# Four channel blocks of a depthwise convolution as fused multiply-adds on VectorE alone, in a two-block transformer on one core

## The chip, the core and the metric

The kernel runs on one core of a Trainium2 chip. The metric is the device time of one execution in microseconds; lower is better. A core has TensorE (PE in the rows; its weight loads are PEld), VectorE (DVE), ScalarE (ACT), GpSimd (POOL) and the queue engine SyncE (SP), each with its own queue of instructions that it works off in order, and 16 DMA engines.

## What is computed

Two transformer blocks over 256 tokens of width 1024, in float32. The second block also carries 256 context tokens, and its first mixer has attention on one half of the width and a convolution module on the other half. The change is in that module:

```python
def _conv_module(u, conv_w, conv_b, ln_g, ln_b):
    a, gate = jnp.split(u, 2, axis=-1)
    glu = a * jax.nn.sigmoid(gate)
    y = lax.conv_general_dilated(glu, conv_w[:, None, :], window_strides=(1,),
                                 padding=[(CONV_WIDTH // 2, CONV_WIDTH // 2)],
                                 dimension_numbers=('NWC', 'WIO', 'NWC'),
                                 feature_group_count=B_WIDTH) + conv_b
    ...
    return jax.nn.silu(yn)
```

The convolution is depthwise: each of 512 channels has 31 weights (CONV_WIDTH) of its own, over the 256 tokens. Then follow a layer norm over the channels and a silu. It is done once for x and once for the context.

## The kernel before, in words

Matrix products run as three float32r matmuls: both operands are split into a high and a low part, and hi*hi, hi*lo and lo*hi are summed in PSUM. Weights come through a ring of 1 MB buffers. `Splits.emit` (L281) splits 128x1024 values of weight at a time: ScalarE makes the high part (L300), VectorE subtracts it for the low part (L301); four such split buffers are in use in turn. A matmul on the low part waits for L301.

The stages around the change are these. The first block's second feed-forward layer (`ffn`, L1009) runs 8 chunks: `gemm_T` (L354, matmuls L363 to L365) makes the hidden layer, `gemm` (L306, matmuls L319 to L321) the output, which is added to x by L1040 on VectorE at the end. Between its chunks the function `between` (L2440) already projects the context for the second block's first mixer, class `MixerAB`: its gate, the other half `a` of the gated unit, keys and values, queries. `MixerAB.a` (L1287) makes the gated input GT (L1292) and calls `conv(1)` for the context. After the feed-forward layer x is normed (L456 to L490), `MixerAB.run` (L1385) projects x in the same way, with attention of the context beside it, and `a` calls `conv(0)` for x. Then come the queries and keys of x with their norm and rotation (L390 to L402, L1091 to L1105, L1111, L1127, L1134), attention (scores L1165, row maximum L1176, exponential L1183, transposes L788), and `gated_out` (L1213), which multiplies attention's output and the convolution's by the output weights and needs both.

Channels lie on the partitions, 128 to a block, so a convolution is 4 blocks (k) of 31 taps (j). `tap` (L1304) does one tap of one block over 128x256. The first tap is on ScalarE for all blocks (L1308). A later tap of a block of the engine "vector" is one scalar_tensor_tensor on VectorE (L1310): y = GT*w + y, the weight being one value per partition. A later tap of a block of the engine "gpsimd" is two instructions: ScalarE scales GT into one of four buffers (L1313) and GpSimd adds that to y (L1314).

```python
CONV = ((0.65, 0.8, 3), (0.4, 0.7, 2))
...
def conv(self, s):
    dve, pool, n = CONV[s]
    self.spare.share = dict(vector=dve, gpsimd=pool)
    for e, ks in (("vector", range(n)), ("gpsimd", range(n, 4))):
        for j in range(31):
            for k in ks:
                self.spare.add(e, 0.1 if j == 0 else 0.4 if e == "vector" else 0.7,
                               lambda k=k, j=j, e=e: self.tap(s, k, e, j))
        self.spare.add(e, 0.0, lambda: self.half(s))
```

The table CONV (L31; first entry x, second the context) gives the shares of the two engines and n, the number of blocks on VectorE: 3 of 4 for x, 2 of 4 for the context. The taps are put on two lists in `Spare` (L1192). They go into the engines' queues beside the matmuls: the generating code calls `tick` every few matmuls, a tick counts as 1.3 units of time (2.0 while it only waits, and 1.0 more where a step of attention was taken), and `Spare.step` gives each list that time multiplied by its share as credit and takes taps off it while the credit is above zero, at 0.4 a tap for VectorE and 0.7 for GpSimd. So a share sets how many taps stand between two other instructions. When both lists of a stream are done, `lnorm` (L1331) is started: transposes of y (L1339), moments (L1345), scaling (L1353), transposes back (L1362), silu (L1369 to L1373) and the split into hi and lo (L1377, L1378) for the output product, each step some ticks after the one before (STEP: 1 for x, 3 for the context).

Of the kernel before, what the change touches and what calls it, by code (L numbers as in the profile page):

```python
# [27 lines left out]
RINGS = (4, 3, 1)  # L28
OVER = 7
EXTRA = (1, 0)  # L30
CONV = ((0.65, 0.8, 3), (0.4, 0.7, 2))  # L31
STEP = (1, 3)


# [93 lines left out]
def body(tc, d, dump=None):  # L128
    nc = tc.nc
    es = ExitStack()  # L130
    with es:
# [1100 lines left out]
        class MixerAB:  # L1232
# [83 lines left out]
# [9 lines that stand above are left out]
# [1218 lines left out]
```

## Time and profile before

| | us |
|---|---|
| median of 3 runs (2215.06 to 2218.03) | 2217.5 |
| the profiled execution, its own time | 2219.68 |
| its span, first to last instruction | 2217.9 |
| TensorE busy | 2010.5 (91%) |
| VectorE busy | 1037.8 (47%) |
| ScalarE busy | 773.9 (35%) |
| GpSimd busy | 487.4 (22%) |

Times in rows are microseconds from the span's start; ns where marked or where a mean of one instruction is given. A busy share over the whole span is an average over stages with different limits. In a row of the table by stage the pairs are busy time and number of instructions, in the order TensorE, weight loads, VectorE, ScalarE, GpSimd; the granted clock is the share of TensorE's full clock that it was given. A row of a group names line, engine, operation, the tile written and the tiles read, the shape and the count; then busy time and mean of one; then the idle time of the engine just before such instructions and what ended it. In the timeline, "x7" are seven instructions run one after the other in the length given; an idle time before them stands in brackets with its releaser.

### The profile page before, as it was taken

How to read it: one execution, taken by the hardware profiler on the slowest of the kernel's cores; microseconds unless marked ns; L12 is line 12 of the kernel's file. 1: busy time of each engine (PE TensorE's matmuls, PEld its weight loads, DVE VectorE, ACT ScalarE, POOL GpSimd, SP SyncE). 2: the span in 40 equal slices, each digit the busy share in tenths (PEclk: the TensorE clock that was granted, in tenths of full speed). 3: DMA queues.
4: the chain of work that ended last, by engine and by line, in shares of the span. 5: the costliest groups of instructions: out<-in, count | busy, mean ns of one | idle time of the engine just before them, and what ended most of it. 6: DMA issues, size and time to landing. Idle time of an engine off the chain costs nothing. (4 is left out here: it accounts for less than half of the span.)

```text
span 2217.9 us, 28427 instructions
## 1 busy us (share of the span) xinstructions
PE 2010.5 (91%) x10991; PEld 1273.2 (57%) x10991; DVE 1037.8 (47%) x2033; ACT 773.9 (35%) x1379; POOL 487.4 (22%) x443
## 2 busy tenths in 40 slices
PE   7998999997998798579899998999798799998998
PEld 5765888774898686357444454444375534443333
DVE  5744554654658955875633232333463422222222
ACT  5544544555666556554211111111264311111110
POOL 3000110100115610403232332332340111111111
PEclk8998999998999998788999999999999899999999
DMA  9775677675554342114699997999742699999998
GB/s 321 271 262 202 237 249 258 208 266 173 176 194 152 126 159 78 56 48 161 236 420 414 411 413 298 416 416 412 279 152 109 236 420 421 421 421 383 421 421 340
DMA packets 160766, 613.00 MB, mean 276 GB/s; under 512 B 10527, under 2 KB 16255, under 8 KB 111344
## 3 DMA queue, kind: packets, MB, share of 16 engines
q1 hardware_dynamic: 155744, 596.86, 69.9%
q0 software_dynamic: 4448, 13.51, 2.2%
q8 instruction: 89, 1.46, 0.3%
q10 hardware_dynamic: 432, 0.74, 0.1%
q14 instruction: 53, 0.43, 0.1%
HBM read 607.90 MB, written 3.16 MB: 276 GB/s over the span
## 5 line engine op out<-in xcount | busy, mean ns | idle before, releaser
L1966 PE MATMUL acc<-w,XT 128*64 128x512 f32 x1856 | 437.2, 600 | 18.8 <-DVEq L2233 10.7
L301 DVE TENSOR_TENSOR w<-w 128x1024 fp32r<-128x1024 f32 x244 | 307.0, 1271 | 193.8 <-ACT w L300 172.5
L300 ACT ACTIVATE w<-w 128x1024 fp32r<-128x1024 f32 x252 | 265.0, 1059 | 184.8 <-PE acc L321 93.2
L1966 PEld LDWEIGHTS acc<-w,XT 128*64 128x64 f32 x1856 | 139.0, 138 | 282.6 <-issue 253.5
L2025 POOL TENSOR_TENSOR X<-X,tm 128x512 f32<-128x512 f32 x124 | 155.3, 1280 | 424.9 <-DVE tm L2023 424.9
L2023 DVE TENSOR_TENSOR tm<-acc,gate 128x512 f32<-128x512 f32 x196 | 129.6, 686 | 217.9 <-PE acc L2013 172.2
L2004 PE MATMUL acc<-w,hT 128*64 128x512 f32 x912 | 215.8, 598 | 6.0 <-ACT hT L1992 6.0
L363 PE MATMUL acc<-hi,w 128*128 128x256 f32 x576 | 166.4, 289 | 8.1 <-ACT qn L1102 3.8
L364 PE MATMUL acc<-lo,w 128*128 128x256 f32 x576 | 164.1, 285 | 0.8 <-POOL lo L490 0.8
L365 PE MATMUL acc<-hi,w 128*128 128x256 f32 x576 | 164.0, 285 | 0.6 <-DVE w L301 0.6
L321 PE MATMUL acc<-w,lo 128*128 128x512 f32 x368 | 150.6, 409 | 1.8 <-POOL lo L1378 1.6
L319 PE MATMUL acc<-w,hi 128*128 128x512 f32 x336 | 143.5, 427 | 7.0 <-ACT hi L1377 5.5
L320 PE MATMUL acc<-w,hi 128*128 128x512 f32 x336 | 137.6, 409 | 9.8 <-DVE w L301 9.8
L2025 POOL TENSOR_TENSOR C<-C,tm 128x512 f32<-128x512 f32 x64 | 79.5, 1275 | 273.8 <-DVE tm L2023 273.8
L1992 ACT ACTIVATE hT<-trp 128x512 f32<-128x512 f32 (+1 forms) x33 | 19.6, 592 | 329.3 <-PE trp L1989 329.3
L1983 DVE SCALAR_TENSOR_TENSOR hd<-sg,ws,acc 128x512 f32<-128x512 f32 (+1 forms) x33 | 36.3, 1100 | 195.9 <-issue 99.4
L2004 PEld LDWEIGHTS acc<-w,hT 128*64 128x64 f32 x912 | 62.7, 136 | 110.5 <-issue 99.0
L363 PEld LDWEIGHTS acc<-hi,w 128*128 128x128 f32 x576 | 111.3, 193 | 10.8 <-ACT qn L1102 4.0
L1314 POOL TENSOR_TENSOR cy<-cy,tap 128x256 f32<-128x256 f32 x90 | 88.1, 998 | 120.0 <-ACT tap L1313 70.6
L365 PEld LDWEIGHTS acc<-hi,w 128*128 128x128 f32 x576 | 112.5, 195 | 0.8 <-DVE w L301 0.8
L2136 PE MATMUL acc<-P,hi 128*128 128x256 f32 x544 | 104.5, 291 | 8.9 <-issue 6.6
L364 PEld LDWEIGHTS acc<-lo,w 128*128 128x128 f32 x576 | 111.4, 193 | 1.4 <-POOL lo L490 1.1
(425 smaller groups left out, 3521.3 us busy)
## 6 DMA issues: line engine op xcount, KB each, us to landing
w<-in_ex_gate_dram SPq DMA_DIRECT2D x118, 1024.0 KB, 13.3
w<-in_ex_up_dram SPq DMA_DIRECT2D x118, 1024.0 KB, 14.3
w<-in_ex_down_dram SPq DMA_DIRECT2D x118, 1024.0 KB, 13.1
w<-in_ffn_w_dram SPq DMA_DIRECT2D x64, 1024.0 KB, 5.2
fw<-in_mod_w_dram SPq DMA_DIRECT2D x48, 1024.0 KB, 7.5
w<-in_a_w_qkv_dram SPq DMA_DIRECT2D x17, 1024.0 KB, 10.3
w<-in_w_in_ab_dram SPq DMA_DIRECT2D x14, 1024.0 KB, 5.3
w<-in_b_w_qkv_dram SPq DMA_DIRECT2D x12, 1024.0 KB, 5.7
```

The costliest lines, as they stand in the source:

```text
L300: nc.scalar.activation(wh, w, AF.Copy)
L301: self.engine.tensor_tensor(wl, w, wh.bitcast(F32), op=OP.subtract)
L319: nc.tensor.matmul(ps[:, :n], xh, wh, start=first, stop=False)
L320: nc.tensor.matmul(ps[:, :n], xh, wl, start=False, stop=False)
L321: nc.tensor.matmul(ps[:, :n], xl, wh, start=False, stop=last)
L363: nc.tensor.matmul(z, wh[:, js], xh, start=k == 0 and j % 2 == 0, stop=False)
L364: nc.tensor.matmul(z, wh[:, js], xl, start=False, stop=False)
L365: nc.tensor.matmul(z, wl[:, js], xh, start=False, stop=k == 7 and j % 2 == 1)
L1966: nc.tensor.matmul(p[self.rows(a)], self.XT[:, 4 * k0 + k, self.rows(a)], units[v + a][:, k], start=k0 + k == 0, stop=4 * k0 + k == 7)
L2004: nc.tensor.matmul(self.p[c][self.rows(a)], self.hT[:, 2 * n + k, self.rows(a)], units[v + a][:, k, s], start=n + k == 0, stop=n + k == 2)
L2023: nc.vector.tensor_tensor(g, p, gates[s][:, c], op=OP.mult)
L2025: add.tensor_tensor(dst, dst, g, op=OP.add)
```

## The change

It alters the table of shares and nothing else in the source: all four blocks are put on VectorE's list, GpSimd's list holds only the call that counts it as done, and VectorE's share goes from 0.65 to 0.85 for x and from 0.4 to 0.5 for the context.

```diff
-CONV = ((0.65, 0.8, 3), (0.4, 0.7, 2))
+CONV = ((0.85, 0.1, 4), (0.5, 0.1, 4))
```

With it the 90 instructions of L1313 and the 90 of L1314 are gone, and 90 of L1310 come in. What the new shares do to the order shows in three places.

GpSimd's queue, from the context's gated input to the output product (L1025 squares the hidden layer, L490 and L1378 split, L674 loads gates, L1220 adds the output to the stream):

```order
 L1290 MEMSET GT 128x4x15
-L1314 TENSOR_TENSOR cy<-cy,tap 128x256 x11
-L1025 TENSOR_TENSOR s<-r 128x512 x2
-L1314 TENSOR_TENSOR cy<-cy,tap 128x256 x26
-L1025 TENSOR_TENSOR s<-r 128x512 x2
-L1314 TENSOR_TENSOR cy<-cy,tap 128x256 x23
-L1025 TENSOR_TENSOR s<-r 128x512 x2
```

The 60 adds of the context leave the queue, and the squares follow one another; the 30 of x go in the same way.

VectorE's queue in the last chunks of the feed-forward layer, after the second query tile of the context (L1088), where before the context's last two FMAs and then only splits stood:

```order
 L1088 TENSOR_TENSOR qr<-qn,gain_5311 128x2x4x64
 L301 TENSOR_TENSOR w<-w 128x1024
+L1310 SCALAR_TENSOR_TENSOR cy<-GT,cols,cy 128x256 x3
+L301 TENSOR_TENSOR w<-w 128x1024
+L1310 SCALAR_TENSOR_TENSOR cy<-GT,cols,cy 128x256 x3
+L301 TENSOR_TENSOR w<-w 128x1024
+L1310 SCALAR_TENSOR_TENSOR cy<-GT,cols,cy 128x256 x3
+L301 TENSOR_TENSOR w<-w 128x1024
+L1310 SCALAR_TENSOR_TENSOR cy<-GT,cols,cy 128x256 x5
+L1031 TENSOR_TENSOR hl<-s,hh 128x512
```

Up to the place of the context's last FMA before there are now 76 FMAs in place of 60; the other 44 go between the splits of the rest of the layer, one to five at a time, and the layer norm of the context (L1345 and on) moves behind the first addition into x (L1040).

VectorE's queue in the stretch of x, around the second query tile:

```order
-L1310 SCALAR_TENSOR_TENSOR cy<-GT,cols,cy 128x256 x6
+L1310 SCALAR_TENSOR_TENSOR cy<-GT,cols,cy 128x256 x9
 L586 TENSOR_REDUCE hss<-qr 128x8
 L390 TENSOR_SCALAR nv<-hss 128x8
 L301 TENSOR_TENSOR w<-w 128x1024
-L1310 SCALAR_TENSOR_TENSOR cy<-GT,cols,cy 128x256 x3
+L1310 SCALAR_TENSOR_TENSOR cy<-GT,cols,cy 128x256 x4
 L397 RECIPROCAL rstd<-sd 128x8
```

Each burst of FMAs between the other instructions of that stretch is longer by up to three; 13 of the 30 more stand before the place that ran at 944, 17 after it.

## Rows read from the trace of the kernel before

**Rows 1.** the page, part 1: busy time, share of the span, instructions of each engine.

```profile
PE 2010.5 (91%) x10991; PEld 1273.2 (57%) x10991; DVE 1037.8 (47%) x2033; ACT 773.9 (35%) x1379; POOL 487.4 (22%) x443
```

**Rows 2.** table by stage; columns: length, busy by engine, TensorE's granted clock, DMA share, GB/s.

```profile
681.00:782.00 101.00, 77.04 (x429) 66.15 (x428) 94.65 (x116) 61.23 (x113) 68.44 (x64) 0.90 0.39 125
782.00:826.60 44.60, 44.60 (x266) 40.09 (x266) 25.31 (x36) 26.77 (x39) 8.76 (x6) 0.96 0.48 156
826.60:893.00 66.40, 55.68 (x417) 48.43 (x416) 36.83 (x69) 41.14 (x89) 2.71 (x4) 0.90 0.32 104
893.00:944.00 51.00, 25.74 (x111) 16.51 (x110) 46.96 (x94) 28.17 (x65) 25.15 (x31) 0.73 0.10 39
944.00:982.00 38.00, 33.00 (x207) 22.45 (x205) 33.74 (x80) 18.73 (x40) 3.54 (x4) 0.93 0.20 70
```

**Rows 3.** groups by line, TensorE, 681 to 826.6; busy and mean | idle before, releaser.

```profile
L320 PE MATMUL acc<-w,hh 128*128 128x512 f32 x69 | 28.9, 420 | 11.0 <-DVE w L301 11.0
L1339 PE MATMUL trp<-cst,cy 128*128 128x128 f32 x8 | 1.9, 360 | 4.6 <-DVE cy L1310 4.6
```

**Rows 4.** groups by line, VectorE, 681 to 790.

```profile
L1310 DVE SCALAR_TENSOR_TENSOR cy<-GT,cols,cy 128x256 f32<-128x256 f32 x60 | 44.5, 781 | 0.1
L301 DVE TENSOR_TENSOR w<-w 128x1024 fp32r<-128x1024 f32 x25 | 38.6, 1542 | 10.4 <-ACT w L300 10.4
```

**Rows 5.** groups by line, VectorE, 790 to 890.

```profile
L301 DVE TENSOR_TENSOR w<-w 128x1024 fp32r<-128x1024 f32 x25 | 31.0, 1254 | 30.8 <-ACT w L300 30.5
```

**Rows 6.** groups by line, VectorE, 944 to 982.

```profile
L1310 DVE SCALAR_TENSOR_TENSOR cy<-GT,cols,cy 128x256 f32<-128x256 f32 x49 | 20.3, 485 | 0.0
```

**Rows 7.** timeline, VectorE; columns: start, length, instruction, count, idle before it.

```profile
747.63 0.97 DVE L1310 SCALAR_TENSOR_TENSOR cy<-GT,cols,cy 128x256 f32<-128x256 f32 x1
748.52 1.76 DVE L301 TENSOR_TENSOR w<-w 128x1024 fp32r<-128x1024 f32 x1
...
958.10 2.85 DVE L1310 SCALAR_TENSOR_TENSOR cy<-GT,cols,cy 128x256 f32<-128x256 f32 x7
```

**Rows 8.** GpSimd: the adds of L1314 (shortest/median/longest), then their group in 681 to 790.

```profile
L1314 POOL TENSOR_TENSOR cy<-cy,tap x90: 720/911/2082, 684.2 to 943.2; 128x256 f32<-128x256 f32 x90
...
L1314 POOL TENSOR_TENSOR cy<-cy,tap 128x256 f32<-128x256 f32 x60 | 63.0, 1079 | 48.1 <-ACT tap L1313 48.0
```

**Rows 9.** groups by line, VectorE, 782 to 826.6.

```profile
L301 DVE TENSOR_TENSOR w<-w 128x1024 fp32r<-128x1024 f32 x14 | 17.7, 1279 | 16.8 <-ACT w L300 16.5
L1373 DVE SCALAR_TENSOR_TENSOR yo<-yt,yo 128x512 f32<-128x512 f32 x2 | 1.4, 688 | 0.0
L1345 DVE BATCH_NORM_STATS2 yst<-yt 128x6 f32<-128x512 f32 x2 | 1.4, 686 | 0.0
```

**Rows 10.** groups by line, VectorE, 890 to 944.

```profile
L1310 DVE SCALAR_TENSOR_TENSOR cy<-GT,cols,cy 128x256 f32<-128x256 f32 x42 | 22.4, 589 | 0.2 <-ACT cy L1308 0.2
```

**Rows 11.** timeline, VectorE: the first and the second query tile.

```profile
913.34 0.20 DVE L397 RECIPROCAL rstd<-sd 128x8 f32<-128x8 f32 x1
919.51 2.45 DVE L1310 SCALAR_TENSOR_TENSOR cy<-GT,cols,cy 128x256 f32<-128x256 f32 x6
...
927.62 0.19 DVE L397 RECIPROCAL rstd<-sd 128x8 f32<-128x8 f32 x1
931.88 1.66 DVE L1310 SCALAR_TENSOR_TENSOR cy<-GT,cols,cy 128x256 f32<-128x256 f32 x4
```

**Rows 12.** timeline, TensorE: matmuls that waited.

```profile
836.84 1.97 PE L478 MATMUL trp<-cst,xn 128*128 128x128 f32 x8 [2.46 <-ACT xn L462]
...
981.01 1.39 PE L1339 MATMUL trp<-cst,cy 128*128 128x128 f32 x4 [3.15 <-DVE cy L1310]
998.61 0.79 PE L319 MATMUL acc<-w,hi 128*128 128x512 f32 x1 [5.25 <-ACT hi L1377]
```

**Rows 13.** groups by line, ScalarE, 681 to 1010.

```profile
L1313 ACT ACTIVATE tap<-GT,cols 128x256 f32<-128x256 f32 x90 | 40.8, 500 | 3.9 <-POOL cy L1314 3.8
```

**Rows 14.** the page, part 2: GB/s moved in 40 slices of 55.4 us.

```profile
GB/s 321 271 262 202 237 249 258 208 266 173 176 194 152 126 159 78 56 48 161 236 420 414 411 413 298 416 416 412 279 152 109 236 420 421 421 421 383 421 421 340
```

## Prediction

> **What bounds the kernel now.** Over the whole span TensorE is busy 91% and VectorE (DVE in the rows) 47% [rows 1]. Neither average says anything about the convolution, which lives in two short stretches, so I cut the span there and read the table by stage [rows 2]. From 681 to 782 us the context's convolution runs under the feed-forward layer's matmuls: VectorE is busy 94.7 of 101 us, TensorE only 77.0, at a granted clock of 0.90. From 782 to 826.6 the same layer goes on without convolution, and TensorE is busy all 44.6 us. From 893 to 982 the convolution of x runs; VectorE has 47.0 of 51 and then 33.7 of 38 us, and TensorE 25.7 of 51.
>
> What TensorE waits for there says the same: from 681 to 826.6 it stood 11.0 us for L301, VectorE's half of a weight split, and 4.6 us for the last fused multiply-add (FMA) of L1310 [rows 3]. So VectorE is the bound in the first and third stretch. The transfers are not: the slices of the two stretches, the 13th to 18th, moved 152 down to 48 GB/s, later ones 412 to 421 [rows 14].
>
> Next I read what VectorE spends there. An FMA took 44.5/60 = 0.74 us from 681 to 790 [rows 4], but 20.3/49 = 0.41 us after 944 [rows 6], when GpSimd (POOL) no longer adds. The timeline shows it singly: 0.97 us for one FMA at 747.63, 2.85 us for seven at 958.10 [rows 7]. Splits too: 25 took 38.6 us beside the adds and 25 took 31.0 after them [rows 4, 5]. GpSimd's 60 adds ran 63.0 us in that first stretch [rows 8]. I read this as VectorE and GpSimd holding each other up.
>
> **The change, part by part.** It removes 90 adds on GpSimd and 90 scalings on ScalarE, 40.8 us of its busy time [rows 13], and adds 90 FMAs on VectorE: 60 for the context, 30 for x. All FMAs go out on a new schedule of ticks.
>
> *Context, to 782.* The order of the change has 76 FMAs up to the place of the last one before, where 60 stood. VectorE now needs 94.65 us. The FMAs give back 44.5 - 60 x 0.41 = 19.9, the splits 38.6 - 31.0 = 7.6; the 16 more cost 6.6. That leaves 73.8. TensorE's own work is 77.04 x 0.90 = 69.3 at full clock, a little less, so VectorE stays the bound. Its idle time was 6.35 us, mostly waiting for ScalarE's half of the split [rows 4]; ScalarE loses 60 x 0.50 = 30 of 61.2 us, so I take half, 3. The stretch goes from 101 to 77: **-24**. Ends: TensorE's floor and 1 us, 70 (-31); VectorE with twice its idle time, 86.5 (-14.5).
>
> *Context, 782 to 826.6.* Here 44 FMAs are new, 18.0 us, and the layer norm behind them moves on, of which L1373 and L1345 show 2.8 us [rows 9]. VectorE needs 25.3 + 18.0 - 2.8 = 40.5, TensorE 44.60 x 0.96 = 42.8. TensorE's work hides it, but closely. I take **+2**; ends 0, and +7, which is all the idle time VectorE had before (6.35) put behind its 40.5 and some clock lost.
>
> *The norm moved.* It lands between 826.6 and 893, where x's own norm makes TensorE wait already, 2.46 us at L478 [rows 12]. Most of the moved work has room (VectorE 36.8, ScalarE 41.1 of 66.4 us). I take **+2**, about one such wait; ends 0 and +7, three of them.
>
> *x, 893 to 982.* VectorE gets 30 x 0.41 = 12.3 us more. It gets back 22.4 - 42 x 0.41 = 5.2 on the FMAs [rows 10] and 6.17 - 4.26 = 1.9 on one query tile (from L397 to the next FMA beside adds, and without) [rows 11]; for the keys ahead of it I estimate the same 1.9 from that row. Net +3.3. ScalarE loses 15 us here, and of VectorE's 8.3 idle us a part closes: **+1**. Ends: all of the idle time closes, -5; or the 17 FMAs that now stand behind 944, 7 us, come on top and one more, +8. At the end of this stretch the first matmul on y waits for the last FMA (3.15 us), so a longer tail would show directly [rows 12].
>
> GpSimd has nothing late that waits on the removed adds, and its square of relu no longer queues behind them; I count nothing for that. The split buffers' transfers are issued as buffers come free, and with under 0.5 of the DMA engines' time used they follow [rows 2].
>
> Sum: -24 + 2 + 2 + 1 = **-19 us**. Against the profiled execution's 2219.7 us that is 2200.7; it stands 2.2 above the median of the runs shown, 2217.5, so I forecast **2198.5**. The ends of the terms add to -35.5 and +7.5; they won't all fall together, and I give the forecast -31 to -7, 2186.5 to 2210.5.
>
> **Where a rule speaks to it.** The timeline shows FMAs and splits, which both read two SBUF tiles, at 0.97 instead of 0.41 us and at 1.76 [rows 7]. The Trainium skill, SBUF — State Buffer, section Who interferes with whom, says that a VectorE instruction with two SBUF inputs and a GpSimd instruction that reads SBUF exclude each other, the later one blocked for the whole of the other. The rows bear out the exclusion; by the strict form each add would give VectorE its whole length back, which is the rival of the larger gain below. The same skill, Perfetto Trace Analysis, section Optimizing Scalar/DVE Operations, says that work may be moved off a saturated VectorE, to ScalarE or even GpSimd, though it doubts the latter for the port they share. Taken by its first half it speaks against this change; what that would cost is the first slower rival.
>
> **The rivals.**
>
> *It isn't the adds that stretch the FMAs* (slower). Then nothing comes back: +6.6 to 782, +2, +2, and +12.3 for x, 23 us, 2240.5. For it: adds and scalings stop at the same time, so the trace can't part them by that alone. Against: both go. It decides at an FMA of 0.50 us: the first stretch is then 45.6 + 76 x 0.50 = 83.6 (-17.4), the second spills 2 more, x costs 120 x 0.09 = 10.8 more, and the sum is 0.
>
> *Splits wait in the queue behind FMAs* (slower). TensorE may wait because of what stands ahead of a split on VectorE's in-order queue, not because VectorE is full. Its 24.0 idle us over 25 splits are 0.96 each; if these stay and the 14 splits to 826.6 [rows 9] get the same, behind up to five FMAs, the cost is 13.4 + 2 + 1 = 16 us, 2233.5. Against: the wait is seen only where VectorE has no free time. It decides at 0.78 us a split: 112.1 + 39 x 0.78 = 142.5, which is 145.6 less the other terms.
>
> *The gain is given back* (no change). A stream of weights that ran ahead could end at the same time whatever came before: 2217.5. Against: the transfers stand nearly still just before the experts' weights come [rows 14], so that stream starts when this stage lets it.
>
> *A larger gain.* If each add took its shortest time, 0.72 us [rows 8], from VectorE, 60 give 43 us back and the first stretch is at TensorE's floor, -31; x gets 21.6 for 12.3, -9. With the other two terms -36: 2181.5. Against: the measured differences come to 27.5 there, not 43.
>
> **How the numbers follow.** A measurement of this kernel can tell about 0.2%, 4.4 us, from no change. Chances: the forecast 0.65, the larger gain 0.10, given back 0.08, not the adds 0.09, splits held 0.08. That makes 0.75 faster, 0.08 the same and 0.17 slower. The range goes from 2184, which leaves out half of the larger gain, to 2230, which reaches into the lower part of the slower cases: about 0.05 and 0.12 left out.
>
> **What would show it.** Right: FMAs at about 0.41 us everywhere, 240 in all and no L1314; splits near 1.24 us; 681 to the first addition into x (L1040, at 826.6) some 20 us shorter, with VectorE over nine tenths busy to its end and TensorE above 85%; x's stretch as long as before. Wrong: FMAs at 0.5 us or more; TensorE waiting for L301 past the old 782; a norm of the context that holds up the first matmuls on x; or both stretches shorter and the end unmoved.

## The result, and the profile after

The changed kernel takes **2187.43 us** (median of 4 runs, 2184.34 to 2190.46); the kernel before, measured beside it, 2216.28 (4 runs, 2214.45 to 2218.03). The ratio is 0.9878, 95% interval 0.9866 to 0.9890: by it 27 us faster (the two medians lie 28.9 apart). The forecast was 2198.5, the range 2184 to 2230. The execution with the profile took 2184.34 us, span 2182.6.

The page of the kernel after, part 1 (answers to [rows 1]):

```profile
PE 1986.8 (91%) x10991; PEld 1262.9 (58%) x10991; DVE 1037.2 (48%) x2123; ACT 734.8 (34%) x1287; POOL 399.3 (18%) x353
```

VectorE runs 90 instructions more in the same busy time, 1037.2 us against 1037.8. GpSimd loses 88 us and ScalarE 39. VectorE's busy time shows no gain at all; the place where its work stands does.

To see it, both traces are cut at the same instructions: the context's gated input GT (first start of L1292), the first addition into x (L1040), the gated input of x (L1292 again), and the end of the last FMA. The table by stage of the kernel before, with the cuts moved to these places (columns as in [rows 2]):

```profile
680.90:826.60 145.70, 121.74 (x694) 106.34 (x693) 120.06 (x153) 87.99 (x152) 77.20 (x70) 0.92 0.41 135
826.60:891.10 64.50, 53.78 (x401) 46.53 (x400) 35.10 (x66) 40.00 (x86) 2.71 (x4) 0.89 0.32 105
891.10:981.60 90.50, 60.25 (x330) 40.58 (x329) 82.06 (x176) 48.03 (x106) 28.69 (x34) 0.82 0.16 53
```

The same of the kernel after:

```profile
672.30:790.30 118.00, 110.72 (x681) 98.16 (x680) 111.37 (x195) 57.76 (x76) 10.49 (x8) 0.99 0.52 168
790.30:857.70 67.40, 54.96 (x420) 47.68 (x420) 40.19 (x83) 44.04 (x99) 4.51 (x5) 0.92 0.29 98
857.70:946.90 89.20, 59.61 (x326) 41.25 (x325) 84.36 (x207) 36.59 (x77) 5.44 (x5) 0.83 0.16 54
```

The context's stretch goes from 145.7 to 118.0 us: -27.7. VectorE is now busy 94% of all of it, and TensorE 94% at a granted clock of 0.99 instead of 84% at 0.92. On TensorE the 27.7 us are 16.7 of idle time (24.0 before, 7.3 after) and 11.0 of busy time, for nearly the same matmuls at a higher granted clock. The stretch of x's norm is 2.9 us longer and the stretch of x's convolution 1.3 shorter. From the start of the last FMA to the first product of the module's output with its gate (L1218; the tail in the table below) it is 25.8 us where it was 24.7, and from there to the end (the rest) 1210.3 where it was 1212.0. So next to nothing of the gain is given back later.

One thing in these two traces is not the change's: the stretch begins at 672.3 instead of 680.9, though the instructions up to there are the same. That start moves from execution to execution, and TensorE's granted clock with it (last section), so the comparison below goes by lengths of stretches.

The groups by line on VectorE in the context's stretch, after (answers to [rows 4, 9]):

```profile
L1310 DVE SCALAR_TENSOR_TENSOR cy<-GT,cols,cy 128x256 f32<-128x256 f32 x120 | 56.8, 523 | 0.1
L301 DVE TENSOR_TENSOR w<-w 128x1024 fp32r<-128x1024 f32 x39 | 48.3, 1240 | 6.6 <-ACT w L300 6.6
```

Before, over the same stretch:

```profile
L301 DVE TENSOR_TENSOR w<-w 128x1024 fp32r<-128x1024 f32 x39 | 56.3, 1448 | 22.9 <-ACT w L300 22.6
L1310 DVE SCALAR_TENSOR_TENSOR cy<-GT,cols,cy 128x256 f32<-128x256 f32 x60 | 44.5, 781 | 0.1
```

120 FMAs take 56.8 us where 60 took 44.5, and the 39 splits take 8.0 us less. On TensorE the waits of [rows 3] are nearly gone:

```profile
L320 PE MATMUL acc<-w,hh 128*128 128x512 f32 x68 | 27.3, 401 | 2.7 <-DVE w L301 2.7
L1339 PE MATMUL trp<-cst,cy 128*128 128x128 f32 x4 | 1.0, 300 | 0.8 <-DVE cy L1310 0.7
```

### The profile page after: what moved, and what is told of

It reads as the page before. It is cut to its first block, busy times and chain, and to the rows that moved or that the text cites. A ratio compares the mean times of both kernels' runs of the same rounds, so it can differ in the third digit from the quotient of the medians.

```text
span 2182.6 us, 28252 instructions
## 1 busy us (share of the span) xinstructions
PE 1986.8 (91%) x10991; PEld 1262.9 (58%) x10991; DVE 1037.2 (48%) x2123; ACT 734.8 (34%) x1287; POOL 399.3 (18%) x353
## 5 line engine op out<-in xcount | busy, mean ns | idle before, releaser
L301 DVE TENSOR_TENSOR w<-w 128x1024 fp32r<-128x1024 f32 x244 | 297.9, 1233 | 172.8 <-ACT w L300 154.9
L363 PE MATMUL acc<-hi,w 128*128 128x256 f32 x576 | 163.9, 285 | 5.4 <-ACT hi L489 2.2
L365 PE MATMUL acc<-hi,w 128*128 128x256 f32 x576 | 161.8, 281 | 0.0
L320 PE MATMUL acc<-w,hi 128*128 128x512 f32 x336 | 137.1, 408 | 8.3 <-DVE w L301 8.2
L363 PEld LDWEIGHTS acc<-hi,w 128*128 128x128 f32 x576 | 108.7, 189 | 8.1 <-ACT hi L489 2.6
L365 PEld LDWEIGHTS acc<-hi,w 128*128 128x128 f32 x576 | 110.1, 191 | 0.0
L417 ACT ACTIVATE Yh<-acc 128x512 fp32r<-128x512 f32 x63 | 37.6, 597 | 209.2 <-PE acc L2004 200.2
```

The costliest lines, as they stand in the source:

```text
L301: self.engine.tensor_tensor(wl, w, wh.bitcast(F32), op=OP.subtract)
L320: nc.tensor.matmul(ps[:, :n], xh, wl, start=False, stop=False)
L363: nc.tensor.matmul(z, wh[:, js], xh, start=k == 0 and j % 2 == 0, stop=False)
L365: nc.tensor.matmul(z, wl[:, js], xh, start=False, stop=k == 7 and j % 2 == 1)
```

## The experiments

Lengths of the stretches in each kernel's profiled execution, in us, between the starts of the instructions named above (the last FMA's start for the third):

| kernel | start of L1292 | context | norm of x | x | tail, to L1218 | rest |
|---|---|---|---|---|---|---|
| before | 680.9 | 145.8 | 64.4 | 90.1 | 24.7 | 1212.0 |
| after | 672.3 | 118.0 | 67.3 | 88.8 | 25.8 | 1210.3 |
| after, again | 673.1 | 118.0 | 67.5 | 88.8 | 25.9 | 1209.7 |
| context only | 672.6 | 117.9 | 67.4 | 91.0 | 24.8 | 1212.0 |
| x only | 677.1 | 145.7 | 64.4 | 87.8 | 25.9 | 1209.9 |
| adds kept | 676.7 | 138.2 | 68.0 | 98.5 | 25.3 | 1211.9 |
| scalings kept | 679.1 | 115.8 | 68.0 | 89.3 | 26.1 | 1211.6 |
| memsets | 681.0 | 118.0 | 67.4 | 88.8 | 25.8 | 1209.9 |
| spread only | 673.1 | 125.6 | 68.0 | 91.1 | 24.1 | 1212.7 |
| dense | 675.5 | 137.3 | 64.3 | 87.8 | 25.8 | 1213.7 |
| share 0.6 | 674.0 | 127.1 | 67.3 | 89.4 | 25.7 | 1211.7 |
| share 0.45 | 680.5 | 114.7 | 69.3 | 90.3 | 26.1 | 1209.3 |
| squares on ScalarE | 682.5 | 113.4 | 68.1 | 88.8 | 26.2 | 1212.0 |

The table CONV in the diffs starts from the changed kernel unless said otherwise.

### Which stream carries it: context only, x only

```diff
-CONV = ((0.85, 0.1, 4), (0.5, 0.1, 4))
+CONV = ((0.65, 0.8, 3), (0.5, 0.1, 4))
```

> All four blocks on VectorE for the context alone; x keeps 3 blocks on VectorE and 1 with scalings and adds. My theory (the adds on GpSimd held up a full VectorE, and the context's FMAs now reach into a stretch where it had room): the context carries nearly the whole gain, 24 to 30 us, so about 2188 to 2193 us, and the stretch from the context's gated input (L1292) to the first addition into x (L1040) is about 118 us as in the change, against 145.8 before. Rival (x's tail gains as much as the context, because its queries and keys no longer stand beside adds): only half of it, 2200 us or more.

Measured: 2187.36 us (2184.55 to 2194.09), ratio to before 0.9881 [0.9859, 0.9903].

```diff
-CONV = ((0.85, 0.1, 4), (0.5, 0.1, 4))
+CONV = ((0.85, 0.1, 4), (0.4, 0.7, 2))
```

> All four blocks on VectorE for x alone; the context as before. My theory: 12.3 us of FMAs come in and about 9 us of held-up time go out, so the time stays within 4 us of before, 2212 to 2220 us. Rival (each add takes its full 0.72 us from VectorE): 9 us faster, 2207 us. Rival (VectorE's longer tail holds the output product): 7 to 12 us slower, 2224 us or more.

Measured: 2212.51 us (2207.95 to 2214.73), ratio 0.9989 [0.9979, 1.0000]. The context's part alone gives the whole gain; x's part alone gives about 2 us, with an interval that reaches to nothing. Of its 2.3 us in the stretch of x the tail takes half back.

### Which of the removed instructions cost the time: adds kept, scalings kept, memsets

The changed kernel with GpSimd adds put back, one for each that was removed, put into its queue at the same taps and written to a buffer that nobody reads (so they cost what they hold up, and nothing waits for their results):

```diff
     nc.vector.scalar_tensor_tensor(v, g, w, v, op0=OP.mult, op1=OP.add)
+    if k >= (3, 2)[s]:
+        nc.gpsimd.tensor_tensor(self.wk.tile([128, 256], F32, name="tap", bufs=4), g, g, op=OP.add)
```

> The change, with one GpSimd addition of the same size (GT + GT, both read from SBUF, into a buffer that nobody reads) beside each of the 90 FMAs that replaced a scaling and an add; no scalings. My theory: each of the 60 adds in the context takes 0.4 to 0.5 us from VectorE, which has no room there, so 20 to 28 us of the gain are lost, and x loses some 9 more: 2210 to 2225 us, with FMAs at 0.6 us or more where adds run. Rival (ScalarE, or the order of the FMAs alone, made the gain): 2185 to 2193 us with FMAs still at 0.41 us.

Measured: 2219.76 us (2217.15 to 2224.38, 7 runs), ratio 1.0021 [1.0009, 1.0032]: the whole gain is gone. The stretch of the context grows by 20.2 us, that of x by 9.7. Table by stage and VectorE's groups in the context's stretch of that kernel, then its adds on GpSimd from 660 to 1010:

```profile
676.70:814.90 138.20, 116.51 (x680) 101.00 (x679) 132.31 (x195) 57.47 (x76) 65.72 (x68) 0.95 0.45 147
```

```profile
L1310 DVE SCALAR_TENSOR_TENSOR cy<-GT,cols,cy 128x256 f32<-128x256 f32 x120 | 72.5, 653 | 0.1
L301 DVE TENSOR_TENSOR w<-w 128x1024 fp32r<-128x1024 f32 x39 | 50.7, 1301 | 4.2 <-ACT w L300 4.2
L1031 DVE TENSOR_TENSOR hl<-s,hh 128x512 fp32r<-128x512 f32 x8 | 8.4, 1045 | 0.0
```

```profile
L1312 POOL TENSOR_TENSOR tap<-GT 128x256 f32<-128x256 f32 x90 | 75.1, 867 | 32.1 <-DVE GT L1292 32.1
```

VectorE runs the same 195 instructions as in the kernel after, and is busy 132.3 us instead of 111.4: 15.7 us more on the FMAs, 2.4 on the splits, 3.0 on L1031. Sixty adds that nobody waits for cost the stretch 20.2 us, 0.34 each, where one lasts 0.87 in the mean. They did it by VectorE and not by GpSimd's queue: GpSimd worked them off in batches of 6 to 20 behind each pair of squares (L1025), and stood idle for over 4 us before every pair in the stretch, so the squares did not wait behind adds. This run isn't the kernel before with another order. It has the adds on top of all 120 FMAs, so it prices an add, and not the exchange of an add for an FMA.

The same with the scalings instead of the adds:

```diff
+    if k >= (3, 2)[s]:
+        nc.scalar.activation(self.wk.tile([128, 256], F32, name="tap", bufs=4), g, AF.Copy, scale=w)
```

> The change, with the 90 scalings on ScalarE left in, written to buffers that nobody reads; GpSimd adds nothing. My theory (contention of VectorE with GpSimd): within 3 us of the change, 2185 to 2191 us. Rival (the gain came from ScalarE, whose half of the weight splits no longer queues behind scalings): it loses 45 us of ScalarE's time again and gives back 10 us or more, 2198 us or more.

Measured: 2188.71 us (2184.72 to 2194.89), ratio 0.9880 [0.9856, 0.9905]. The context's stretch takes 115.8, 2.2 us less than in the change, which was not followed up. ScalarE's lost time was worth nothing here.

And with an instruction on GpSimd that only writes, in place of the add:

```diff
+    if k >= (3, 2)[s]:
+        nc.gpsimd.memset(self.wk.tile([128, 768], F32, name="tap", bufs=1), 0.0)
```

> The change with one GpSimd memset of 128x768 beside each of the 90 FMAs, into a buffer that nobody reads. Theory (VectorE's second SBUF input and GpSimd's reads exclude each other, writes alone don't): FMAs stay at 0.41 to 0.47 us and the time within 4 us of the change, 2184 to 2192 us. Rival (any instruction running on GpSimd holds VectorE up): as with the adds kept, 2205 to 2222 us.

Measured: 2188.75 us (2182.53 to 2192.68), ratio 0.9872 [0.9853, 0.9890]. GpSimd's group from 660 to 830, and VectorE's FMAs in the context's stretch of that kernel:

```profile
L1312 POOL MEMSET tap<- 128x768 f32 x60 | 44.5, 741 | 3.2
```

```profile
L1310 DVE SCALAR_TENSOR_TENSOR cy<-GT,cols,cy 128x256 f32<-128x256 f32 x120 | 56.6, 520 | 0.1
```

Of these 60 memsets, each of the length of a short add, 54 ran in the stretch. They leave the FMAs as they are (56.6 against 56.8 us) and the stretch at 118.0. So GpSimd being busy is not what holds VectorE up: its memsets, which only write, cost nothing, and its adds, which read, do.

### Faster FMAs or other places: spread only, dense

The change does two things: it takes the adds away, and by the share it spreads the taps over the whole rest of the feed-forward layer. The spreading alone, from the kernel before, with its adds and scalings:

```diff
-CONV = ((0.65, 0.8, 3), (0.4, 0.7, 2))
+CONV = ((0.65, 0.8, 3), (0.25, 0.44, 2))
```

> The kernel before with nothing but the context's shares lowered, from 0.4 and 0.7 to 0.25 and 0.44: 2 blocks stay on GpSimd, and the context's taps reach, like the change's, to the first addition into x. Theory 'spread' (VectorE was full for 100 us and half idle for the 45 after; what counts is that its work is laid over the whole stretch): VectorE's need from L1292 to L1040 is 115 to 120 us either way, so the stretch takes 120 to 127 us against 145.8 before and 118.0 in the change, and the time is about 2191 to 2199 us. Theory 'adds' (the gain is the time that the adds no longer take from VectorE): the stretch stays at 135 us or more, 2205 us or more.

Measured: 2196.80 us (2195.07 to 2200.79), ratio 0.9922 [0.9905, 0.9938], some 17 of the 27 us; the context's stretch takes 125.6.

The other half: all taps on VectorE, but put as densely as before, so that they end about where they ended:

```diff
-CONV = ((0.85, 0.1, 4), (0.5, 0.1, 4))
+CONV = ((0.85, 0.1, 4), (0.8, 0.1, 4))
```

> The change with the context's share at 0.8 in place of 0.5: all 120 FMAs on VectorE, in as many ticks as the taps before. Theory 'spread': VectorE needs some 98 us by the tick where it needed 94.7 before, and the room behind stays empty, so the stretch from L1292 to L1040 takes 135 to 146 us and most of the gain is lost, 2204 to 2216 us. Theory 'adds': it keeps the gain, 2185 to 2194 us.

Measured: 2206.03 us (2200.20 to 2206.49), ratio 0.9951 [0.9933, 0.9969]; the context's stretch takes 137.3. Its table by stage, the context's stretch cut after the last FMA:

```profile
675.50:768.40 92.90, 74.82 (x427) 64.10 (x426) 89.54 (x177) 37.38 (x53) 4.89 (x4) 0.92 0.41 136
768.40:812.80 44.40, 44.40 (x269) 39.93 (x269) 25.42 (x38) 26.82 (x40) 8.75 (x6) 0.97 0.48 159
```

This is the picture of [rows 2] again: VectorE full and TensorE waiting, then TensorE full and VectorE at 57%. The four kernels make a square, in us of the context's stretch: 145.8 before; 125.6 with the spreading alone (-20.2); 137.3 with nothing but the adds exchanged for FMAs (-8.5); 118.0 with both (-27.8). The two nearly add up, and **the spreading is the larger part**. The kernel with the spreading alone, its table by stage and VectorE's groups in the context's stretch:

```profile
673.10:798.70 125.60, 113.29 (x681) 98.66 (x680) 116.87 (x136) 80.41 (x136) 78.49 (x68) 0.97 0.50 163
```

```profile
L301 DVE TENSOR_TENSOR w<-w 128x1024 fp32r<-128x1024 f32 x39 | 58.6, 1509 | 6.3 <-ACT w L300 6.3
L1310 DVE SCALAR_TENSOR_TENSOR cy<-GT,cols,cy 128x256 f32<-128x256 f32 x60 | 46.9, 804 | 0.1
```

VectorE's busy time is 116.9 us there, and 120.1 before: it fell by 3, the stretch by 20. The place of the work gave that, not its amount. From here to the change the adds go out and 60 FMAs come in: the splits take 10.3 us less, the FMAs 9.9 more. What the adds held up and what the FMAs cost nearly cancel on these two lines, and so the exchange is worth only 7.6 to 8.5 us of stretch.

### How far to spread: shares 0.6 and 0.45

```diff
-CONV = ((0.85, 0.1, 4), (0.5, 0.1, 4))
+CONV = ((0.85, 0.1, 4), (0.6, 0.1, 4))
```

> The change with the context's share at 0.6 in place of 0.5: the FMAs end some 14 splits before the first addition into x, and the context's norm has more room. Theory 'spread': VectorE is a little too full early, the stretch takes 120 to 126 us, the next one 1 to 3 us less than in the change: 2186 to 2194 us. If the last 20% of spreading does not matter it is 1 to 3 us faster than the change.

Measured: 2197.90 us (2195.30 to 2201.68), ratio 0.9926 [0.9909, 0.9943], the context's stretch 127.1. This missed: the stretch follows the share more steeply than I thought. A third of the way back from 0.5 to 0.8 costs 9.1 of the 19.3 us between them.

```diff
-CONV = ((0.85, 0.1, 4), (0.5, 0.1, 4))
+CONV = ((0.85, 0.1, 4), (0.45, 0.1, 4))
```

> The change with the context's share at 0.45 in place of 0.5: the last 7 FMAs go behind the first addition into x, and the context's norm ends closer to the attention. Theory 'spread': VectorE has a little more room, the stretch from L1292 to L1040 takes 115 to 118 us (112 is TensorE's own work), but the FMAs and the norm now stand in the chain of x's norm, 2 to 4 us longer: 2185 to 2191 us, no clear difference. If the spreading still paid as from 0.6 to 0.5 it would gain 9 us, 2179 us.

Measured: 2187.75 us (2185.02 to 2191.97), ratio 0.9880 [0.9865, 0.9896]. The context's stretch is 3.3 us shorter (114.7), the norm of x 2.0 and its convolution 1.5 longer: what the layer gains, the stages behind it pay. So past 0.5 nothing was left to gain in the sum.

### What still holds the FMAs: squares on ScalarE, and the change once more

GpSimd still squares the hidden layer (L1025, which reads r as both of its inputs). Put on ScalarE:

```diff
-nc.gpsimd.tensor_tensor(s, r, r, op=OP.mult)
+nc.scalar.activation(s, r, AF.Square)
```

> The change with the square of relu (L1025, 8 chunks of two in each feed-forward layer) on ScalarE in place of GpSimd. In the change's trace the FMAs beside these multiplications on GpSimd take 0.7 to 0.95 us instead of 0.41. Theory (two-input reads of VectorE and GpSimd exclude each other, and VectorE is the bound): the FMAs come back to 0.41 to 0.43 us, VectorE gets some 6 us back in the stretch and it goes from 118 to 113 to 116 us; in the other feed-forward layer, where VectorE has room, nothing: 2181 to 2186 us. Rival (ScalarE's 0.6 us a square delay the splits): as the change or slower.

Measured: 2187.31 us (2181.57 to 2193.27, 6 runs), ratio to the kernel before 0.9878 [0.9859, 0.9897]. The time, expected at 2181 to 2186, missed by 1 us; the stretch came out as expected. Table by stage and VectorE's FMAs in its context's stretch:

```profile
682.50:795.90 113.40, 109.06 (x680) 97.41 (x680) 105.18 (x195) 61.99 (x84) 0.00 (x0) 1.00 0.53 175
```

```profile
L1310 DVE SCALAR_TENSOR_TENSOR cy<-GT,cols,cy 128x256 f32<-128x256 f32 x120 | 51.2, 476 | 0.1
```

The FMAs give back 5.6 us and the stretch 4.6. The whole kernel shows no clear difference from the change: the profiled execution began the stretch only at 682.5, and its runs lie 12 us apart. The edit also moves the squares of the chunks ahead of the stretch to ScalarE; whether that costs what the stretch gains is open.

The changed kernel again, beside these, unchanged:

> The change itself once more, beside the two variants that follow. Same as before: 0.984 to 0.990 of the kernel before, about 2187 us, with 118 us from L1292 to the first addition into x. The time at which L1292 starts, which lay between 672 and 681 us in executions with the same instructions up to there, says how much of a difference between two executions is none of the change's.

Measured: 2185.62 us (2182.45 to 2190.68, 5 runs), ratio 0.9876 [0.9858, 0.9894]. The stretches repeat within 0.2 us, and the rest within 0.6. None of the variants run here beats it by what can be measured.

## Why the prediction was right, and where it was too small

**The bound.** Right. VectorE was what the context's stretch waited for: adds on GpSimd that hold it up put the stretch back to 138.2, 60 scalings more on ScalarE don't lengthen it (115.8), and TensorE's wait for the splits (L320) fell from 11.0 to 2.7 us. After the change VectorE and TensorE are both busy 94% of the stretch, so it is no longer VectorE alone that is full.

**The first term, -24.** Right. Cut after the 24th split of the stretch, the end of the old busy part (781.0 before, 748.8 after, with 60 and 76 FMAs ahead of the cut), the pieces are, before:

```profile
680.90:781.00 100.10, 76.14 (x425) 65.25 (x424) 94.75 (x117) 60.79 (x113) 68.44 (x64) 0.90 0.39 127
781.00:826.60 45.60, 45.60 (x271) 41.09 (x270) 25.31 (x36) 27.21 (x40) 8.76 (x6) 0.95 0.47 152
```

After:

```profile
672.30:748.80 76.50, 71.97 (x473) 65.03 (x472) 72.22 (x133) 38.89 (x54) 5.00 (x4) 1.00 0.51 166
748.80:790.30 41.50, 38.75 (x210) 33.13 (x209) 39.15 (x63) 18.88 (x22) 5.48 (x4) 0.96 0.54 172
```

The first piece gave 23.6. VectorE's need, forecast at 73.8 us, was 72.2, and its idle time, taken as 3, was 4.3.

**The second term, +2, is the step that failed.** The piece gave another 4.1 us instead of costing 2, outside the ends that I had given it, 0 and +7. I had taken its old 266 matmuls, 42.8 us at full clock, as a floor under it. But they weren't all its own. The timeline of TensorE before, at the end of the first piece, and then the hidden layer's matmuls in the second piece before and after:

```profile
779.51 1.30 PE L1339 MATMUL trp<-cst,cy 128*128 128x128 f32 x4 [4.56 <-DVE cy L1310]
780.46 0.56 PE L363 MATMUL acc<-hi,w 128*128 128x256 f32 x1
```

```profile
L363 PE MATMUL acc<-hi,w 128*128 128x256 f32 x48 | 14.9, 311 | 0.0
```

```profile
L363 PE MATMUL acc<-hi,w 128*128 128x256 f32 x32 | 9.0, 281 | 0.0
```

Before, TensorE stood 4.56 us for the last FMA, with the transposes of y in its in-order queue ahead of the matmuls of the next hidden layer. With the FMAs spread the transposes come later, sixteen more groups of three such matmuls were done before the cut, and eight transposes of the context's norm (L1362) went behind the piece. So it holds 210 matmuls, 38.75 x 0.96 = 37.2 us at full clock, instead of 271. VectorE's need there was forecast well (40.5; 39.2 measured), and with the floor gone the piece takes 41.5, not much more than that need. The cut lay at a place in VectorE's queue, and TensorE's backlog at that place was read as work of the later piece. The whole stretch taken at once would have avoided it: TensorE's own 121.74 x 0.92 = 112 us for it, VectorE's 73.8 + 40.5 = 114.3, and 118.0 measured.

**0.41 us for an FMA** was too little: 56.8 us for 120 are 0.47. The 0.41 came from long rows of FMAs (seven in 2.85 us [rows 7]). One by itself lasts 0.48 (at 759.00 in the trace after), and after the change they stand in ones to fives. "I count nothing for that" was said of the squares on GpSimd because nothing late waits for them; but they read SBUF too. The timeline after shows the FMAs beside and without a square, then the square on GpSimd:

```profile
748.80 1.27 DVE L1310 SCALAR_TENSOR_TENSOR cy<-GT,cols,cy 128x256 f32<-128x256 f32 x3
...
751.12 2.84 DVE L1310 SCALAR_TENSOR_TENSOR cy<-GT,cols,cy 128x256 f32<-128x256 f32 x3
```

```profile
750.59 2.70 POOL L1025 TENSOR_TENSOR s<-r 128x512 f32<-128x512 f32 x2 [33.96 <-ACT r L1023]
```

The three took 2.84 us instead of 1.27. Without the squares on GpSimd 120 FMAs took 51.2, 0.43 each. The error cost the sum little: VectorE's need came out 1.6 and 1.3 us under the forecast in the two pieces even so, since the other instructions between the FMAs were quicker too. L1088 on the queries, for one, took 0.90 us before and 0.69 after, and such instructions had not been counted.

**The norm, +2**: 2.9 measured. The wait by which I had priced it did not grow. TensorE at L478 after, from the timeline:

```profile
800.87 1.09 PE L478 MATMUL trp<-cst,xn 128*128 128x128 f32 x8 [1.95 <-ACT xn L462]
```

It is 1.95 us after 2.46 [rows 12]. VectorE has 5.1 us more work in the stretch (40.2 against 35.1); which wait carries the 2.9 us was not settled.

**x, +1**: -1.3 in its stretch and +1.1 in the tail, -0.2. VectorE did 30 more FMAs in 2.3 us more of busy time, close to the +3.3 worked out.

**The sum.** Terms as measured: -27.7 + 2.9 - 0.2 - 1.7 (the rest) = -26.7, against the ratio's 27. Forecast -19. Of the 7.7 us between them, 6.1 are the second term, 1.2 x, and 1.7 the rest, which moves by as much in other kernels of the table; 0.4 of the first term and 0.9 of the norm go the other way. So the miss is nearly all in the one step. The lower ends given to the terms add to -36, not -35.5; they held the sum, and the median lies 0.9 us inside the forecast's own range, 2186.5 to 2210.5.

**The rivals.** "It isn't the adds": fallen by the runs with adds and with scalings kept. "Splits wait behind FMAs": fallen, the splits were waited for 2.7 us where there had been 11.0, and up to five FMAs ahead of one cost nothing that shows. "Given back": fallen, the rest is 1210.3 after 1212.0. "A larger gain", VectorE getting back each add's whole 0.72 us: the context came near its size, but by the spreading. In the run with adds kept an add cost 0.34 us, and x gained nothing where this rival had -9. The Trainium skill, SBUF — State Buffer, section Summary: rules for kernel authors, says that of two such instructions the later one is fully blocked. An add that comes second would then cost VectorE nothing, which fits a loss of two fifths of its length, though no run here parts the cases. The Trainium skill, on the same page, section Who interferes with whom, also says that a GpSimd instruction that only writes doesn't contend with a two-input VectorE one; the memsets agree (118.0 us with and without).

**What the reasons got wrong together.** The prediction told the gain as 27.5 us that GpSimd gives back on FMAs and splits, less 6.6 for more FMAs. The four kernels of the square tell it the other way: 20.2 of the 27.8 us are to be had by the spreading alone, with not one instruction moved to another engine. The arithmetic had this in it (only 16 of the 60 new FMAs were charged to the first piece, 44 put into VectorE's free time behind it), but as a side condition, where it was the main effect. At its own prices the exchange by itself, 27.5 us back for 60 FMAs at 0.41, is worth 2.9 us; it measured 7.6 to 8.5.

## What to carry to other kernels

Before moving work to another engine, look for a neighbouring stretch where the full engine is idle and nothing needs the result early: here the same work put more thinly gave three quarters of the gain in the stretch (20.2 of 27.8 us). When a stretch is cut for a prediction, check on each engine whether the work behind the cut was late or belongs there, or take both pieces as one. And price work on GpSimd by what it holds up on VectorE as well as by who waits for it: an add that nobody read cost 0.34 us of a stretch in which VectorE was full.

## What was not expected of the hardware

- GpSimd instructions that only write left VectorE alone: 54 memsets of 0.74 us in the stretch, and FMAs of 56.6 us against 56.8. Sixty adds with two reads cost 15.7 us on the FMAs.
- The start of the context's stretch, behind instructions that are the same in all these kernels (but for six memsets that GpSimd ran early in that run), lay between 672.3 and 681.0 us in 12 profiled executions (the run with squares on ScalarE, which changes them, left out), while the stretches behind it repeat within 0.2 us (the change, twice, and the run with memsets). TensorE's granted clock goes with it. Up to that start it was 0.98 in the six executions that began the stretch by 675.5, 0.97 in the six that began it from 676.7 on, and 0.96 with the squares on ScalarE (682.5). Whole times follow it too: in the run with memsets 2182.53 us at a mean granted clock of 0.965, and 2192.68 at 0.959. What lets the clock differ between executions of the same instructions is open. The difference is larger than several effects sought here, so lengths between two instructions of one trace told more than whole times.
